# The products' weights at the start of their tile: an encoder block on one Trainium2 core

## The chip, the cores and the metric

The kernel runs on one core of one Trainium2 chip. The metric is the time of one execution on the device, in microseconds (us). Three executions of the kernel before took 967.39, 967.70 and 967.99 us; the median is 967.7. One further execution was profiled.

The names of the profile are used throughout. PE is TensorE's matmul part and PEld its part that loads the stationary operand (the weights of the array); DVE is VectorE, ACT is ScalarE, POOL is GpSimd, and SP issues most of the DMAs. A matmul holds one operand still in the array (the stationary one, 128 x 128 here) and lets the other stream past it (the moving one, 512 or 256 columns here). PSUM is the memory that matmuls write to, SBUF the one that they read from. A line number as L1014 is that of the kernel's source.

## What is computed

One layer of an encoder over 256 positions and 2048 features: a mixing half (windowed attention and a Fourier group) and a feed-forward half. The change lies in the feed-forward half:

```python
D_MODEL, SEQ = 2048, 256
D_FF = 5504

def _conv_ffn(h, w_up, dw_w, dw_b, w_down):
    up = h @ w_up
    gate, val = up[..., :D_FF], up[..., D_FF:]
    gate = lax.conv_general_dilated(gate, dw_w, ..., feature_group_count=D_FF) + dw_b
    act = jax.nn.gelu(gate, approximate=False) * val
    return act @ w_down

x = x + jnp.concatenate([a, f], axis=-1) @ w_out
x = x + _conv_ffn(_rmsnorm(x, norm2_g), w_up, dw_w, dw_b, w_down)
return _rmsnorm(x, normf_g)
```

All inputs and the output are float32.

## The kernel before

**Matmuls by parts.** The matmuls of the large projections work on float32r, a type in which PE streams one column of the moving operand after the other in a single pass. To keep the accuracy of float32, each operand is split into a high part (`hi`, the value copied to float32r) and a low part (`lo`, what the copy lost), and three of the four partial products are summed: high by high, low by high, high by low. ScalarE writes `hi`, VectorE subtracts and writes `lo`. For weights both go into one tile of the tag `parts`, of which there are three buffers, taken in turn (L139). A tile holds 2 x 2048 + 128 elements a partition: the high part in its first half, the low part in its second, and 128 spare elements. So each part can begin some elements in from the start of its half. `PLACES` (L136) gives these two offsets, in elements of 4 bytes, by the kind of unit:

- `still`, offsets 0 and 16: weights that are the stationary operand (query and key projections, and all up tiles). `still_weights` (L315) runs for each of 16 blocks a matmul of 512 columns with the high part (L320; the moving operand is the high and low part of the activations side by side) and one of 256 columns with the low part (L321).
- `first`, offsets 16 and 16: the first eight units, in which the weights are the moving operand.
- `moving`, offsets 0 and 0: the other units with moving weights: the output projection (`ps_a`, `ps_ff`) and the later parts of the down projection (`ps_l`, `ps_e`). `moving_weights` (L303) runs three matmuls of 512 columns a block (L309 to L311).
- `product`, offsets 28 and 28: the weights of the products, below.

**The feed-forward half.** The 43 blocks of 128 hidden features each have a gate tile and a value tile, 5504 = 43 x 128. Such an up tile is one unit of 1 MB of weights and 16 pairs of matmuls. The first 32 blocks form four groups of eight. For each group the down projection is not done as a plain matrix product: the group's activations, its weights and the output are cut into 2 x 2 blocks, and seven products of sums of blocks take the place of eight (Strassen's scheme in the form of Winograd). This is done for two halves of the output's columns, which makes 14 products a group and 56 in all. `by_parts` (L1010) runs a product: four blocks, each with three matmuls of 512 columns: L1014 (high operand, high weights), L1015 (low operand, high weights), L1016 (high operand, low weights). The operand `op` (from the activations) is stationary, the weights are the moving operand. The names of the products are P1, P2, P6, P7, N3, N4 and N5; the profile groups their tiles as `parts_P`, `parts_N`, `op_P`, `op_N`, `ps_P` and `ps_N`.

`split_product` (L904) makes the parts of a product's weights: a copy on ScalarE (L910) and a subtraction on VectorE (L911), then it starts the DMA or the accumulating DMA that prepares a later product's weights. Its source is one raw block of the weights or the tile `sumw`, in which sums of blocks are built.

**The order.** The order of work is written out by hand. The sixteen up tiles of the first eight blocks go first. Then come four stages; each runs the 14 products of a group of eight blocks together with the 16 up tiles of the next eight. `PATTERN` (L61) sets the order in a stage: three up tiles, then 13 times a product and an up tile, then a product. So 19 up tiles run ahead of the first product. At each item the parts of the item two places ahead are made (`ff_step`, L941), so that each writer waits for the buffer of `parts` that the item before has freed. Behind the four stages follow four units of the late down projection (`ps_l`), the last six up tiles, four more units `ps_l`, and the last down units (`ps_e`) with the final normalisation.

Of the kernel before, what the change touches and what calls it, by code (L numbers as in the profile page):

```python
# [83 lines left out]
def block_kernel(  # L84
# [48 lines left out]
    raws, halves = {}, {}  # L133


    PLACES = {"still": (0, 16), "first": (16, 16), "moving": (0, 0), "product": (28, 28)}  # L136

    def parts_tile(name, place):
        t = wp.tile([P, 2 * 2048 + 128], F32R, tag="parts", name=name, bufs=3)  # L139
        oh, ol = PLACES[place]  # L140
        return t[:, oh : oh + 2048], t[:, 2048 + ol : 4096 + ol]

    def load(i, pieces=1):
        if i < len(units) and i not in raws:
            src, n, _ = units[i]
            raws[i] = wp.tile([P, 2048], F32, tag="raw", name=f"raw{i}", bufs=RAW)
            m = n // pieces
            for p in range(pieces):
                s = slice(p * m, (p + 1) * m)
                nc.sync.dma_start(raws[i][:, s], src[:, s])  # L150
                yield
# [50 lines left out]
    first = load(0, 4)  # L202
# [1077 lines left out]
```

## Time and profile before

| | |
|---|---|
| median of three executions | 967.7 us |
| the profiled execution | 967.03 us |
| its span, first to last instruction | 965.3 us |
| mean granted clock of TensorE | 0.998 |
| up tiles alone, then the four stages of products with up tiles | about 260 to 367 us, 367 to 864 us of the span |
| HBM traffic | 208.65 MB read, 2.10 MB written |

The span is the time between the first and the last instruction of the profiled execution; what lies around it belongs to the execution as well. The busy time of an engine is the sum over its instructions. Records of matmuls overlap, since the next one begins to stream while the last one's results still drain; the time that a matmul costs is therefore not its record's duration but the step from its start to the next one's start. Rows in order of time give the start, the duration, the engine, the line and the tile; a row of a group gives the count, the busy time, the mean duration in nanoseconds and the idle time before its instructions.

### The profile page before, as it was taken

How to read it: one execution, taken by the hardware profiler on the slowest of the kernel's cores; microseconds unless marked ns; L12 is line 12 of the kernel's file. 1: busy time of each engine (PE TensorE's matmuls, PEld its weight loads, DVE VectorE, ACT ScalarE, POOL GpSimd, SP SyncE). 2: the span in 40 equal slices, each digit the busy share in tenths (PEclk: the TensorE clock that was granted, in tenths of full speed). 3: DMA queues.
4: the chain of work that ended last, by engine and by line, in shares of the span. 5: the costliest groups of instructions: out<-in, count | busy, mean ns of one | idle time of the engine just before them, and what ended most of it. 6: DMA issues, size and time to landing. Idle time of an engine off the chain costs nothing.

```text
span 965.3 us, 12801 instructions
## 1 busy us (share of the span) xinstructions
PE 955.1 (99%) x5089; PEld 820.1 (85%) x5089; DVE 745.0 (77%) x924; ACT 540.0 (56%) x654; POOL 44.6 (5%) x59
## 2 busy tenths in 40 slices
PE   9999999999999999999999999999999999999996
PEld 7789998888888888888888888888888888888885
DVE  5668877666576689787898877988778979878674
ACT  6756766554455446556565555665555655553534
POOL 0000000000000000000000000000000000000003
PEclk9999999999999999999999999999999999999999
DMA  8854444446456676977778787876977686775532
GB/s 320 338 189 155 175 138 168 142 167 215 177 177 243 233 220 194 288 226 256 225 253 240 235 293 231 261 236 206 290 245 245 206 278 213 227 225 210 209 132 88
DMA packets 33548, 211.59 MB, mean 219 GB/s; under 512 B 3792, under 2 KB 4304, under 8 KB 9424
## 3 DMA queue, kind: packets, MB, share of 16 engines
q1 hardware_dynamic: 29744, 184.54, 51.8%
q0 software_dynamic: 3600, 26.22, 14.5%
q8 instruction: 40, 0.66, 0.3%
q14 instruction: 20, 0.16, 0.0%
q10 hardware_dynamic: 144, 0.01, 0.0%
HBM read 208.65 MB, written 2.10 MB: 218 GB/s over the span
## 4 chain that ended last, share of the span: by engine, by line
PE 98%; DMA 1%; ACT 0%; SPq 0%; POOL 0%; issue 0%; DVE 0%; ACTq 0%; POOLq 0%
PE ps_val L320 16%; PE ps_gate L320 16%; PE ps_gate L321 8%; PE ps_val L321 8%; PE ps_q L320 5%; PE ps_P L1015 3%; PE ps_P L1014 3%; PE ps_P L1016 3%; PE ps_N L1015 2%; PE ps_q L321 2%; PE ps_N L1014 2%; PE ps_a L311 2%; PE ps_a L309 2%; PE ps_a L310 2%; PE ps_N L1016 2%; PE ps_k L320 2%
## 5 line engine op out<-in xcount | busy, mean ns | idle before, releaser
L171 DVE TENSOR_TENSOR parts<-raw,parts 128x2048 fp32r<-128x2048 f32 (+3 forms) x145 | 313.0, 2159 | 63.7 <-ACT parts L170 63.5
L170 ACT ACTIVATE parts<-raw 128x2048 fp32r<-128x2048 f32 (+3 forms) x144 | 262.0, 1819 | 75.4 <-PE ps_l L311 25.7
L320 PE MATMUL ps_gate<-hU,parts 128*128 128x512 f32 x688 | 242.2, 394 | 0.0
L320 PE MATMUL ps_val<-hU,parts 128*128 128x512 f32 x688 | 242.2, 394 | 0.0
L321 PE MATMUL ps_gate<-hU,parts 128*128 128x256 f32 x688 | 192.7, 280 | 0.0
L321 PE MATMUL ps_val<-hU,parts 128*128 128x256 f32 x688 | 192.7, 280 | 0.0
L320 PEld LDWEIGHTS ps_val<-hU,parts 128*128 128x128 f32 x688 | 129.3, 188 | 29.8
L320 PEld LDWEIGHTS ps_gate<-hU,parts 128*128 128x128 f32 x688 | 129.3, 188 | 29.7
L321 PEld LDWEIGHTS ps_gate<-hU,parts 128*128 128x128 f32 x688 | 129.2, 188 | 1.1
L321 PEld LDWEIGHTS ps_val<-hU,parts 128*128 128x128 f32 x688 | 129.1, 188 | 1.1
L805 ACT ACTIVATE ft_g<-ps_gate 128x256 f32<-128x256 f32 x43 | 16.6, 385 | 124.2 <-PE ps_gate L321 124.2
L805 ACT ACTIVATE ft_v<-ps_val 128x256 f32<-128x256 f32 x43 | 16.6, 386 | 97.5 <-PE ps_val L321 97.5
L320 PE MATMUL ps_q<-hT,parts 128*128 128x512 f32 x192 | 66.9, 393 | 0.0
L321 PE MATMUL ps_q<-hT,parts 128*128 128x256 f32 x192 | 53.2, 277 | 0.0
L1015 PE MATMUL ps_P<-parts_P,op_P 128*128 128x512 f32 x128 | 50.9, 398 | 0.0
L1014 PE MATMUL ps_P<-parts_P,op_P 128*128 128x512 f32 x128 | 50.2, 392 | 0.0
L1016 PE MATMUL ps_P<-parts_P,op_P 128*128 128x512 f32 x128 | 49.6, 387 | 0.0
L911 DVE TENSOR_TENSOR parts_N<-sumw,parts_N 128x2048 fp32r<-128x2048 f32 x16 | 36.6, 2290 | 10.1 <-ACT parts_N L910 10.1
L320 PEld LDWEIGHTS ps_q<-hT,parts 128*128 128x128 f32 x192 | 36.1, 188 | 7.3
L807 DVE TENSOR_TENSOR fa_g<-ps_gate,ft_g 128x256 f32<-128x256 f32 x43 | 18.1, 421 | 29.0 <-ACT ft_g L805 29.0
L1015 PE MATMUL ps_N<-parts_N,op_N 128*128 128x512 f32 x96 | 38.2, 398 | 0.0
L309 PE MATMUL ps_a<-parts,cat 128*128 128x512 f32 x96 | 37.9, 395 | 0.0
(323 smaller groups left out, 1591.9 us busy)
## 6 DMA issues: line engine op xcount, KB each, us to landing
raw<-in_w_up SPq DMA_DIRECT2D x86, 1024.0 KB, 5.0
raw<-in_w_in SPq DMA_DIRECT2D x21, 1024.0 KB, 5.0
raw<-in_w_out SPq DMA_DIRECT2D x16, 1024.0 KB, 4.8
sumw<-in_w_down POOLq DMA_DIRECT2D x16, 1024.0 KB, 8.6
raw<-in_w_down_late SPq DMA_DIRECT2D x8, 1024.0 KB, 4.8
raw<-in_w_down_last SPq DMA_DIRECT2D x4, 768.0 KB, 4.3
raw<-in_w_in SPq DMA_DIRECT2D x8, 256.0 KB, 6.6
xs<-in_x SPq DMA_DIRECT2D x4, 512.0 KB, 10.7
```

Source lines behind the costliest of these rows:

```text
L170: nc.scalar.activation(hi[:, s], raw[:, s], AF.Copy)
L171: nc.vector.tensor_tensor(lo[:, s], raw[:, s], f32(hi[:, s]), ALU.subtract)
L309: nc.tensor.matmul(ps, ah, wh, start=first and q == q0, stop=False)
L310: nc.tensor.matmul(ps, al, wh, start=False, stop=False)
L311: nc.tensor.matmul(ps, ah, wl, start=False, stop=last and q == q0 + len(kk) - 1)
L320: nc.tensor.matmul(ps, hi[:, s], h, start=k == 0, stop=False)
L321: nc.tensor.matmul(ps[:, 0:S], lo[:, s], h[:, 0:S], start=False, stop=k == NK - 1)
L805: nc.scalar.activation(tmp, ps[:, S : 2 * S], AF.Copy)
L911: nc.vector.tensor_tensor(lo, src, f32(hi), ALU.subtract)
L1014: nc.tensor.matmul(ps, o[:, 0, p, :], hi[:, s], start=first and p == 0, stop=False)
L1015: nc.tensor.matmul(ps, o[:, 1, p, :], hi[:, s], start=False, stop=False)
L1016: nc.tensor.matmul(ps, o[:, 0, p, :], lo[:, s], start=False, stop=last and p == 3)
```

## The change

The offsets of the kind `product` go from 28 to 0 elements, for the high and for the low part. The tile, its size, its buffers, and the offsets of all other kinds stay.

```diff
-    PLACES = {"still": (0, 16), "first": (16, 16), "moving": (0, 0), "product": (28, 28)}
+    PLACES = {"still": (0, 16), "first": (16, 16), "moving": (0, 0), "product": (0, 0)}
...
     def parts_tile(name, place):
         t = wp.tile([P, 2 * 2048 + 128], F32R, tag="parts", name=name, bufs=3)
         oh, ol = PLACES[place]
         return t[:, oh : oh + 2048], t[:, 2048 + ol : 4096 + ol]
```

## The prediction

> **What bounds the kernel now.** I read the page first, then the stages, then TensorE's instructions in order of time.
>
> ```profile
> span 965.3 us, 12801 instructions
> ...
> PE 955.1 (99%) x5089; PEld 820.1 (85%) x5089; DVE 745.0 (77%) x924; ACT 540.0 (56%) x654; POOL 44.6 (5%) x59
> ...
> PE 98%; DMA 1%; ACT 0%; SPq 0%; POOL 0%; issue 0%; DVE 0%; ACTq 0%; POOLq 0%
> ...
> 492.90:621.00 128.10, 128.10 (x680) 109.66 (x679) 106.93 (x109) 72.48 (x70) 5.26 (x6) 1.00 0.79 246
> 621.00:749.30 128.30, 128.30 (x681) 109.82 (x680) 107.21 (x109) 72.69 (x70) 5.25 (x6) 1.00 0.79 245
> ```
>
> The first three lines are the page's span, its busy times and its chain of waits. The last two come from the view by stages: start and end of the second and third group, length, then busy time of PE, PEld, DVE, ACT and POOL, then the granted clock and DMA. In these groups PE never stops, its clock is at full, VectorE works 107 of 128 us and ScalarE 73. So the time is the number of matmuls times the step from one to the next, and no other engine's gain or loss reaches the end unless it makes PE wait. The step is therefore what has to be read closely.
>
> ```profile
> 367.31 0.39 PE L1014 MATMUL ps_P<-parts_P,op_P 128*128 128x512 f32 x1
> 367.55 0.40 PE L1015 MATMUL ps_P<-parts_P,op_P 128*128 128x512 f32 x1
> 367.78 0.39 PE L1016 MATMUL ps_P<-parts_P,op_P 128*128 128x512 f32 x1
> ...
> 370.09 0.39 PE L320 MATMUL ps_val<-hU,parts 128*128 128x512 f32 x1
> ...
> 375.69 0.39 PE L1014 MATMUL ps_P<-parts_P,op_P 128*128 128x512 f32 x1
> ...
> 476.17 0.39 PE L1014 MATMUL ps_N<-parts_N,op_N 128*128 128x512 f32 x1
> ```
>
> These are PE's rows in order of time: start, duration, line. A product (12 matmuls of 512 columns) runs from 367.31 to 370.09: 2.78 us, a mean step of 0.231. The up tile behind it (16 pairs of 512 and 256 columns) runs to 375.69: 5.60 us, 0.350 a pair. 13 such product-and-tile periods end at 476.17: 108.86 / 13 = 8.37 us each, so the two numbers hold throughout. Now the same shapes after the groups, where the moving operand already lies without offset:
>
> ```profile
> 864.22 0.40 PE L309 MATMUL ps_l<-parts,act 128*128 128x512 f32 x1
> ...
> 866.54 0.39 PE L310 MATMUL ps_l<-parts,act 128*128 128x512 f32 x1
> ...
> 885.75 0.39 PE L309 MATMUL ps_l<-parts,act 128*128 128x512 f32 x1
> ...
> 886.43 0.39 PE L320 MATMUL ps_gate<-hU,parts 128*128 128x512 f32 x1
> ...
> 887.47 0.39 PE L320 MATMUL ps_gate<-hU,parts 128*128 128x512 f32 x1
> ...
> 891.89 0.39 PE L320 MATMUL ps_val<-hU,parts 128*128 128x512 f32 x1
> ...
> 919.09 0.39 PE L309 MATMUL ps_l<-parts,act 128*128 128x512 f32 x1
> ...
> 920.25 0.39 PE L311 MATMUL ps_l<-parts,act 128*128 128x512 f32 x1
> ...
> 920.48 0.39 PE L309 MATMUL ps_l<-parts,act 128*128 128x512 f32 x1
> ```
>
> Three steps from 885.75 to 886.43 take 0.68: 0.227 each, against 0.231 in the products. And five up tiles from 891.89 to 919.09 take 27.20: 5.44 each, 0.340 a pair, against 0.350, with the same hU, the same parts buffers, the same place and nothing waited for. So a pair has two paces, and which one it runs at is not fixed by its own addresses; it is handed on from the matmuls before. The groups' tiles are all on the slow one:
>
> ```profile
> L320 PE MATMUL ps_gate<-hU,parts 128*128 128x512 f32 x144 | 50.9, 396 | 0.0
> ...
> L320 PE MATMUL ps_gate<-hU,parts 128*128 128x512 f32 x48 | 16.5, 389 | 0.0
> ...
> 272.03 0.47 PE L320 MATMUL ps_gate<-hU,parts 128*128 128x512 f32 x1
> ```
>
> The first two are the gate's groups of instructions from 271.8 to 367 us and from 886.6 to 919 us: 396 ns a record ahead of the first product, 389 behind the last. The third row is where the slow pace begins: a record of 0.47 us behind four small matmuls. From there nothing interrupts PE, and the products with their offset of 28 do not lead it out.
>
> **The change, part by part.** It removes and adds no instruction, no wait and no DMA; the tile, its three buffers and the order stay. 112 bytes fall away from the address of both parts of a product's weights: ScalarE's write (L910), VectorE's read and write (L911), and the moving operand of L1014 to L1016. In the built program of before, the parts' three buffers begin at bytes 93984, 110880 and 127776 of a partition, all 288 past a multiple of 512; so do the operands' tiles, the act tiles and the cat tiles that are loaded as stationary weights, while the hT tiles are 96 past one. A product's moving rows thus go from 400 to 288, the same remainder as the weights loaded beside them. That is just the case of ps_l (moving 288, weights 288), so its rows price the products.
>
> Products, 56 of them: settled, 12 steps of 0.227 are 2.72 us. Coming from a fast up tile they start unsettled: from 919.09 to 920.25 the first five steps take 1.16 where settled ones take 1.13, so 0.03 more. 2.75 against 2.78 saves 0.03, times 56 is 1.7 us. Bounds for this step: settled from the first (0.06 saved, 3.4 us), or never (below).
>
> Up tiles behind the first product: four groups of 16 are 64, less the three ahead of the first product, 61. If a settled product hands the fast pace on, as ps_l does at 886.43, each saves 5.60 - 5.44 = 0.16, or 9.8 us. The way back into the pace costs: three pairs from 886.43 to 887.47 take 1.04 against 1.02, so 0.02 for each of the 55 tiles that follow a product directly, 1.1 us. Bounds: all 61 fast (9.8), or none (0).
>
> The first product meets a tile on the slow pace, for which no row exists. The nearest is ps_l at 864.22, which follows a product of offset 28: its first ten steps, to 866.54, take 2.32, 0.05 more than settled, and then it is settled. A product has twelve steps, so I take it that the first one, or at worst one of the next, gets through.
>
> The writers: is either slower at the new place?
>
> ```profile
> L171 DVE TENSOR_TENSOR parts<-raw,parts 128x2048 fp32r<-128x2048 f32 x130 | 297.3, 2287 | 56.0 <-ACT parts L170 55.9
> L170 ACT ACTIVATE parts<-raw 128x2048 fp32r<-128x2048 f32 x130 | 248.9, 1915 | 60.8 <-PE ps_l L311 16.8 <-PE ps_a L311 14.2 <-PE ps_ff L311 9.2
> ...
> L911 DVE TENSOR_TENSOR parts_N<-sumw,parts_N 128x2048 fp32r<-128x2048 f32 x16 | 36.6, 2290 | 10.1 <-ACT parts_N L910 10.1
> ...
> L910 ACT ACTIVATE parts_N<-sumw 128x2048 fp32r<-128x2048 f32 x16 | 30.6, 1911 | 0.0
> ```
>
> The offset-free and offset forms differ by 4 ns, at most 56 x 0.004 = 0.2 us on engines with 16 to 43% idle: nothing on the path. What hides the writers is that they run two items ahead of PE. A faster PE eats into that cover. Its thinnest place:
>
> ```profile
> 817.32 2.28 DVE L911 TENSOR_TENSOR parts_N<-sumw,parts_N 128x2048 fp32r<-128x2048 f32 x1
> ...
> 820.05 0.39 PE L1016 MATMUL ps_N<-parts_N,op_N 128*128 128x512 f32 x1
> ```
>
> After eight sums in a row VectorE ends these low parts at 819.60; PE reads them first at 820.05, 0.45 later. In the two tiles and the product ahead of it PE will gain about 0.16 + 0.03 + 0.16 = 0.35, so some 0.1 is left. Should it be gone, PE waits a tenth or two, and one tile may fall back to the slow pace (0.16): under 0.4 us, in the range. VectorE's 107 us still fit in the new group, 128.3 less about 2.6.
>
> Sum: 1.7 + 9.8 - 1.1 = 10.4 us. The profiled execution took 967.03 us (965.3 span and 1.7 around it), 0.7 under the median of 967.7 of the runs shown; on that scale 967.7 - 10.4 = **957.3 us**. With rows to 0.01 us, 56 and 61 times, and with the entry costs dropped (13.2 in all) or doubled (about 7.6), the likeliest case alone lies from 954.5 to 960.
>
> A rule of the Trainium skill speaks against all this. "TensorE: Matmul & The Clock Gate", Step-by-step: what each phase is for, says that PE reads the moving operand and the weights through two independent ports, and that "Loading the next tile's weights doesn't steal SBUF read bandwidth from the running matmul." By it, where the operands lie could not matter and the change would be worth 0 us. The trace does not agree as far as it shows: 0.340 and 0.350 for the same pair, 0.227 and 0.231 for the same shape.
>
> **The rivals.** *The tiles fall back.* The products settle but each gate or value tile returns to 0.350. Against it: 886.43 to 891.89, where the tile stays fast. For it: 272.03, where a fast stage went slow behind other matmuls. Then every product enters from the slow side and costs 2.77: 56 x 0.01, 967.1 us.
>
> *Half.* The pace is lost at waits or some entries and won back only later; about half the tiles gain: 967.7 - 5.2 = 962.5 us.
>
> *No effect of the place.* The two paces come from something that the change does not touch, and the products' 0.231 is their own: 967.7 us. For it: nothing in the page names addresses. Against it: the late products of the same shape, with another place, do not show them.
>
> *Slower: the products lock on their longest step.* The hi and lo operands are 2048 bytes apart here, 1024 in act and cat. If that keeps moving rows and loaded weights colliding when both have the remainder 288, all twelve steps could be as long as the longest of now:
>
> ```profile
> L1014 PE MATMUL ps_P<-parts_P,op_P x128: 392/392/393, 367.3 to 855.2; 128*128 128x512 f32 x128
> ...
> L1015 PE MATMUL ps_P<-parts_P,op_P x128: 398/398/398, 367.5 to 855.4; 128*128 128x512 f32 x128
> ...
> L1016 PE MATMUL ps_P<-parts_P,op_P x128: 387/387/388, 367.8 to 855.6; 128*128 128x512 f32 x128
> ```
>
> These rows of the view of the tile give the shortest, median and longest record. Steps go with these durations: the longest is 6 ns above the mean of 392. 12 x 0.006 x 56 adds 4.0 us, with the tiles still slow: 971.7 us. It decides as soon as the mean step passes 0.231. Against it: the three buffers of the parts lie at different multiples of 512 from the weights, and over all of them the shortest and longest record of a line are 0 or 1 ns apart, so a multiple of 512 between two operands counts for nothing here.
>
> **How the numbers follow.** The forecast 0.74, half 0.08, falling back 0.08, no effect 0.05, slower 0.05. A measurement of this kernel tells about 0.2% (1.9 us) from no change: the first two are faster (0.82), the next two the same (0.13), the last slower (0.05). The range from 954.5 to 963.5 holds the forecast with both its bounds, and the half case.
>
> **What would show it.** Right: L1014 to L1016 all near 389 ns once settled, L320 of the groups near 389 instead of 395, a product-and-tile period of 8.21 us, and the first ps_l some 10 us earlier. If the products show 389 but L320 stays at 395, the handing on failed; if L1014 to L1016 keep 392, 398 and 387, the place is not what sets them; if all show 398, they locked. Idle time on PE in the groups would mean that VectorE's cover broke.

## The result and the profile after

| | before | after |
|---|---|---|
| median | 967.85 us (967.39 to 968.18, 4 runs) | 957.66 us (957.35 to 959.19, 4 runs) |
| ratio | 1 | 0.9898, 95% interval 0.9881 to 0.9915 |
| span of the profiled execution | 965.3 us | 957.4 us |

The change saves 10.2 us, 1.0%; 957.3 had been forecast. The same page of the kernel after, its span, busy times and chain of waits:

```profile
span 957.4 us, 12801 instructions
...
PE 947.1 (99%) x5089; PEld 814.9 (85%) x5089; DVE 745.3 (78%) x924; ACT 540.2 (56%) x654; POOL 44.6 (5%) x59
...
PE 93%; DMA 3%; DVE 1%; ACT 1%; issue 1%; SPq 0%; POOL 0%; ACTq 0%; POOLq 0%
```

The same instructions, the same work on the other engines, and 8 us less on PE. The profiled execution of after is the longest of the four, and its chain holds more DMA than before (3% against 1%): its first loads came later, so that its first product starts at 369.31 us instead of 367.31. That lies ahead of what the change touches: in a second profile of the same kernel the first product starts at 367.58 us. What the change does is read behind that point. PE in order of time (start, duration, line), from the first product on:

```profile
369.31 0.40 PE L1014 MATMUL ps_P<-parts_P,op_P 128*128 128x512 f32 x1
...
372.08 0.39 PE L320 MATMUL ps_val<-hU,parts 128*128 128x512 f32 x1
...
377.54 0.39 PE L1014 MATMUL ps_P<-parts_P,op_P 128*128 128x512 f32 x1
...
380.28 0.39 PE L320 MATMUL ps_gate<-hU,parts 128*128 128x512 f32 x1
...
385.75 0.39 PE L1014 MATMUL ps_N<-parts_N,op_N 128*128 128x512 f32 x1
...
476.02 0.39 PE L1014 MATMUL ps_N<-parts_N,op_N 128*128 128x512 f32 x1
...
856.36 0.39 PE L309 MATMUL ps_l<-parts,act 128*128 128x512 f32 x1
```

The first product takes 2.77 us (before 2.78), the tile behind it at once 5.46 instead of 5.60. The second product takes 2.74. 13 periods of a product and a tile end at 476.02: 106.71 / 13 = 8.21 us, against 8.37. From the first product to the first `ps_l` it is 487.05 us against 496.91 (864.22 less 367.31 in the rows of before): 9.9 us of the 10.2 lie in this stretch.

The records say the same. The gate's group of instructions (count, busy time, mean ns), first of before from 367.3 to 864.2 us, then of after from 369.3 to 856.3 us; behind them the products' lines of after in the view of the tile (shortest, median and longest record):

```profile
L320 PE MATMUL ps_gate<-hU,parts 128*128 128x512 f32 x481 | 169.7, 395 | 0.0
```

```profile
L320 PE MATMUL ps_gate<-hU,parts 128*128 128x512 f32 x481 | 165.7, 390 | 0.0
```

```profile
L1014 PE MATMUL ps_P<-parts_P,op_P x128: 388/393/399, 369.3 to 847.5; 128*128 128x512 f32 x128
L1015 PE MATMUL ps_P<-parts_P,op_P x128: 388/390/398, 369.5 to 847.7; 128*128 128x512 f32 x128
L1016 PE MATMUL ps_P<-parts_P,op_P x128: 388/390/397, 369.8 to 847.9; 128*128 128x512 f32 x128
```

The tiles' 512-column matmuls went from 395 ns to 390. The products no longer repeat one pattern of 392, 398 and 387; they run from 388 to 399, since each begins unsettled and settles on the way.

The thinnest place of VectorE's cover did break, by a little. VectorE's and PE's rows of after there:

```profile
810.55 2.28 DVE L911 TENSOR_TENSOR parts_N<-sumw,parts_N 128x2048 fp32r<-128x2048 f32 x1
```

```profile
812.53 0.40 PE L1015 MATMUL ps_N<-parts_N,op_N 128*128 128x512 f32 x1
812.89 0.51 PE L1016 MATMUL ps_N<-parts_N,op_N 128*128 128x512 f32 x1
```

The low parts are ready at 812.83, and the step to the matmul that reads them is 0.36 instead of about 0.23. This product takes 3.02 us by its starts, 0.27 more than the others: 0.13 is the wait, the rest lies in the steps behind it, which are longer again. The tile behind the product, at 5.47, comes back to the fast pace.

### The profile page after: what moved, and what is told of

It is laid out like the page before. It is cut to its first block, busy times and chain, and to the rows that moved or that the text cites. A ratio compares the mean times of both kernels' runs of the same rounds, so it can differ in the third digit from the quotient of the medians.

```text
span 957.4 us, 12801 instructions
## 1 busy us (share of the span) xinstructions
PE 947.1 (99%) x5089; PEld 814.9 (85%) x5089; DVE 745.3 (78%) x924; ACT 540.2 (56%) x654; POOL 44.6 (5%) x59
## 4 chain that ended last, share of the span: by engine, by line
PE 93%; DMA 3%; DVE 1%; ACT 1%; issue 1%; SPq 0%; POOL 0%; ACTq 0%; POOLq 0%
PE ps_gate L320 16%; PE ps_val L320 16%; PE ps_gate L321 8%; PE ps_val L321 8%; PE ps_q L320 5%; PE ps_P L1015 3%; PE ps_P L1014 3%; PE ps_P L1016 3%; DMA raw<-in_w_in 3%; PE ps_q L321 2%; PE ps_a L311 2%; PE ps_a L309 2%; PE ps_a L310 2%; PE ps_N L1015 2%; PE ps_N L1014 2%; PE ps_N L1016 2%
## 5 line engine op out<-in xcount | busy, mean ns | idle before, releaser
L171 DVE TENSOR_TENSOR parts<-raw,parts 128x2048 fp32r<-128x2048 f32 (+3 forms) x145 | 313.2, 2160 | 63.4 <-ACT parts L170 63.4
L320 PE MATMUL ps_gate<-hU,parts 128*128 128x512 f32 x688 | 238.2, 391 | 0.0
L320 PE MATMUL ps_val<-hU,parts 128*128 128x512 f32 x688 | 238.1, 391 | 0.0
L1015 PE MATMUL ps_P<-parts_P,op_P 128*128 128x512 f32 x128 | 50.2, 392 | 0.0
L1016 PE MATMUL ps_P<-parts_P,op_P 128*128 128x512 f32 x128 | 49.9, 390 | 0.0
L911 DVE TENSOR_TENSOR parts_N<-sumw,parts_N 128x2048 fp32r<-128x2048 f32 x16 | 36.6, 2290 | 10.1 <-ACT parts_N L910 10.1
L1015 PE MATMUL ps_N<-parts_N,op_N 128*128 128x512 f32 x96 | 37.7, 393 | 0.0
```

Of the source, the lines that this page charges most:

```text
L171: nc.vector.tensor_tensor(lo[:, s], raw[:, s], f32(hi[:, s]), ALU.subtract)
L320: nc.tensor.matmul(ps, hi[:, s], h, start=k == 0, stop=False)
L911: nc.vector.tensor_tensor(lo, src, f32(hi), ALU.subtract)
L1015: nc.tensor.matmul(ps, o[:, 1, p, :], hi[:, s], start=False, stop=False)
L1016: nc.tensor.matmul(ps, o[:, 0, p, :], lo[:, s], start=False, stop=last and p == 3)
```

## Experiments

Each run is one profiled execution, with the kernel before timed on the same chip (966.6 to 967.8 us); of e11 five executions were timed, of the kernel after beside it (e12) four. Executions of one kernel lie up to 1.8 us apart, so a small difference between single ones says little; the products and tiles decide. Their times are differences of starts in PE's rows; the first product behind the slow pace and the one that waits for VectorE can be longer than the table has it.

| run | products' offset (high, low), elements | product us | tile us | time us |
|---|---|---|---|---|
| before | 28, 28 | 2.775 | 5.60 | 966.6 to 968.2 |
| after | 0, 0 | 2.745 | 5.46 | 957.7 |
| e1 | 128, 128 | 2.745 | 5.46 | 957.12 |
| e2 | 64, 64 | 2.745 | 5.46 | 958.53 |
| e5 | 32, 32 | 2.80 twice, then 2.78 | 5.60 once, then 5.47 | 960.15 |
| e3 | 16, 16 | 2.75 | 5.60 | 966.56 |
| e6 | 16, 16, operands moved along | 2.746 | 5.454 | 957.50 |
| e9 | 0, 28 | 2.77 to 2.79 | 5.60, 5.44, 5.60 in turn | 965.17 |
| e10 | 28, 128 | 2.78, 2.74 in turn | 5.46, 5.60 in turn | 963.01 |
| e4 | 0 in the first stage, then 28 | 2.745, then 2.720 | 5.46, then 5.440 | 956.40 |
| e7 | 0 in the first product, then 28 | 2.771, then 2.720 | 5.462, then 5.440 | 954.25 |
| e8, e11 | 28, one up tile at 80 | 2.720 | 5.440 | 953.06, 952.29 |

**Is it the remainder, or the start of the tile?** An offset of 128 elements is 512 bytes; 64, 16 and 32 elements, in the other runs, are 256, 64 and 128 bytes.

```diff
-... "product": (0, 0)}
+... "product": (128, 128)}
```

What was expected of e1, e2, e3 and e5, in this order:

> The products' parts lie 128 elements (512 bytes) into their tile instead of 0, so the moving rows have the remainder 288 by 512 again, as the weights loaded beside them. Theory (the place relative to the loaded weights by 512 bytes sets the step): as the kernel after, products with a settled step of 0.227 us and up tiles at 0.340 a pair behind the first product, 957 to 959 us. Rival (the distance from the start of the tile counts, or two writers and readers disturb each other by absolute place): as the kernel before, steps of 0.231 and pairs of 0.350, 967 to 968 us.

> Offset 64 elements, 256 bytes off the remainder of the loaded weights. Theory in its narrow form (only equal remainders by 512 settle at 0.227): a step other than 0.227 and tiles at 0.350, about 967 us. Wide form (a period of 256 or less; the first eight units of the kernel before have moving rows 256 bytes off their weights and settle at 0.227): as the kernel after, 957 to 959 us.

> Offset 16 elements, 64 bytes off. If the period is 64 bytes or less: as the kernel after, 957 to 959 us. If it is larger: a product step of its own, between 0.227 and 0.238, and the up tiles on one of their two paces; at 0.350 a pair about 967 us. Rival (only a start that is a multiple of 64 bytes off matters, as 28 elements are not): 957 to 959 us too, so this run tells only together with the one at 64 elements and those that follow.

> Offset 32 elements, 128 bytes off the loaded weights. The offset of 256 bytes did as 0 did, that of 64 did not. If the period is 128 bytes: as the kernel after, products of 2.745 us and up tiles of 5.46, 957 to 959 us. If it is 256: as at 64 bytes, products of 2.74 to 2.78 us and tiles left at 5.60, about 966.5 us.

512 and 256 bytes did just as 0: products of 2.745 us, tiles of 5.46, first tile behind the first product included. 128 bytes is a place of its own, and neither of its two expectations came true: the first tile behind a product still takes 5.60 us, the second product leads to the fast pace, and from there products take 2.78 us and the tiles behind them 5.47. 64 bytes leaves the tiles on the slow pace with somewhat shorter products. So the start of the tile is nothing special, and the three places 0, 256 and 512 bytes off are alike; those 64, 112 and 128 bytes off are not.

**Is it the place of the moving rows, or of the one operand against the other?** A tile of 16 elements a partition at the head of the feed-forward half's pool moves everything in that pool by 64 bytes. Of what PE reads in the products and the up tiles, only the operands `op` lie there; the products' weights go to offset 16 with them:

```diff
     hT[:] = hT2
+    fp.tile([P, 16], F32, tag="pad", name="pad", bufs=1)
     r2b = fp.tile([P, S], F32, tag="r2b", name="r2b", bufs=1)
...
-... "product": (0, 0)}
+... "product": (16, 16)}
```

What was expected:

> Offset 16 elements as in the run at 966.6 us, but everything of the feed-forward half's own pool, so the operands loaded beside the products' weights too, lies 64 bytes further on: moving rows and loaded weights have one remainder again, 352. Theory (what counts is the place of the one against the other): products settle and lead the tiles to 5.44 to 5.46 us, 957 to 960 us, the late down units (now 64 bytes off their act tiles) perhaps a little slower. Rival (the absolute place of the moving rows counts): products of 2.748 us and tiles of 5.60, about 966.5 us.

PE in order of time, first of e3 (16 elements, operands not moved), then of this run (L1015 is here the product's first line):

```profile
376.66 0.40 PE L1014 MATMUL ps_P<-parts_P,op_P 128*128 128x512 f32 x1
...
379.41 0.39 PE L320 MATMUL ps_gate<-hU,parts 128*128 128x512 f32 x1
...
385.01 0.40 PE L1014 MATMUL ps_N<-parts_N,op_N 128*128 128x512 f32 x1
```

```profile
407.73 0.40 PE L1015 MATMUL ps_P<-parts_P,op_P 128*128 128x512 f32 x1
...
410.48 0.40 PE L320 MATMUL ps_gate<-hU,parts 128*128 128x512 f32 x1
...
415.93 0.40 PE L1015 MATMUL ps_N<-parts_N,op_N 128*128 128x512 f32 x1
```

The product takes 2.75 us in both; the tile takes 5.60 in the one and 5.45 in the other, and the whole 966.56 and 957.50 us. The products' moving rows lie at the same place, and of PE's operands only those loaded beside them have moved. What counts is the place of the one operand against the other. The late down units show it from the other side: in this run their `act` tiles are moved and their weights not, and the four units from the first `ps_l` on take 22.51 us instead of 22.23, the four behind the last up tiles 22.39 instead of 21.79.

**Does every product have to lie there, and does it hand its pace on?** In the first of these runs (e4) only the first stage's products are at 0, in the second (e7) only the very first product.

```diff
-... "product": (0, 0)}
+... "product": (0, 0), "shifted": (28, 28)}
...
-        hi, lo = ... = parts_tile(f"parts_{p}_{g}{c}", "product")
+        hi, lo = ... = parts_tile(
+            f"parts_{p}_{g}{c}", "shifted" if g else "product"
+        )
```

```diff
-            f"parts_{p}_{g}{c}", "shifted" if g else "product"
+            f"parts_{p}_{g}{c}", "product" if (g, c, p) == (0, 0, "P1") else "shifted"
```

What was expected of e4, and then of e7:

> Only the 14 products of the first stage lie without an offset, the other 42 at 28 elements as before. Theory (each product hands its own pace on to the tile behind it, whatever came before): the first stage gains about 2.5 us, and from the first product of the second stage on products step at 0.231 and tiles pair at 0.350, as in the kernel before: 964.5 to 966 us. Rival (one push out of the slow pace is enough, and the fast one then holds): tiles stay at 0.340 in all four stages, only the products' own 0.03 us each are lost: 958.5 to 960.5 us.

> Only the very first product lies without an offset, all 55 others at 28 elements. Theory as it now stands (a product at 28 keeps whichever pace it meets, a product at 0 leads to the fast one): the first takes 2.77 us, all others 2.720, and the tiles 5.440, some 0.6 us less than with the whole first stage at 0: 955.5 to 956.5 us. Rival (one product is too short to settle from the slow pace, its twelve steps being just enough): tiles back at 5.60 behind it, 967 us.

In e4 the theory fell. The rival's mechanism held, the tiles stay fast in all four stages, but not its price: it had the products at 28 lose 0.03 us each and the time at 958.5 to 960.5 us, and they gain instead. The time was 956.40 us, and the stretch from the first product to the first `ps_l` 485.29 us against 487.05 with all products at 0. Rows of PE in e4 (L1016 is here a product's first line), in the first stage at offset 0 and in the second at 28:

```profile
376.49 0.39 PE L1016 MATMUL ps_P<-parts_P,op_P 128*128 128x512 f32 x1
...
379.24 0.39 PE L320 MATMUL ps_gate<-hU,parts 128*128 128x512 f32 x1
...
384.70 0.39 PE L1016 MATMUL ps_N<-parts_N,op_N 128*128 128x512 f32 x1
...
502.22 0.39 PE L1016 MATMUL ps_P<-parts_P,op_P 128*128 128x512 f32 x1
...
504.94 0.39 PE L320 MATMUL ps_gate<-hU,parts 128*128 128x512 f32 x1
...
510.38 0.39 PE L1016 MATMUL ps_N<-parts_N,op_N 128*128 128x512 f32 x1
```

At 0 a product takes 2.75 and the tile 5.46; at 28 they take 2.72 and 5.44, not the 2.78 and 5.60 of the kernel before. A product at 28 has two paces as well, and here it keeps the one that it meets. A product at 0 leads to the fast pace from either, but pays for it each time: 0.025 us in itself and 0.021 in the tile behind. The theory formed from this priced the run with one product at 0 before it ran, at 955.5 to 956.5 us; its products and tiles came out as written (2.771 for the first, then 2.720 and 5.440), and its time, 954.25, a little under: its first product began at 366.69 us, 1.6 us earlier than the 368.26 of e4.

**Is the pace set ahead of all products?** The kernel before with its offsets of 28, and one change: the weights of the third up tile, the one behind the four small matmuls, lie 80 elements in (288 + 320 = 608, remainder 96, as hU's rows).

```diff
-            units.append((w_up[...], 2048, "still"))
+            units.append((w_up[...], 2048, "level" if n == 2 else "still"))
...
-... "product": (28, 28)}
+... "product": (28, 28), "level": (80, 80)}
```

What was expected of the one profile (e8), of its five executions (e11) and of the kernel after beside them (e12):

> The kernel before with all products at 28 elements; only the third up tile's weights (the first tile behind the four small matmuls, where the slow pace begins) lie 80 elements in, so that the loaded weights have the remainder 96 of the moving rows beside them. Theory (equal remainders settle from any start, and everything behind keeps the pace): that tile at 16 x (0.227 + 0.120) = 5.55 us, then 16 more tiles ahead of the first product at 5.44 instead of 5.60, products at 2.720, tiles at 5.44: 967.7 - 2.6 - 3.1 - 9.7 = 952 to 953.5 us. Rival (the tile settles, but the next one with offsets 0 and 16 falls to the slow pace again): 967 us.

> The kernel before with the one up tile at 80 elements again, now timed in five rounds: 952.5 to 953.5 us, a ratio of 0.985 to the kernel before, and 4 to 5 us less than the kernel after.

> The kernel after, timed in five rounds beside it: 957 to 958 us.

PE of e8: the third tile and its successor, then groups of instructions from 278.5 to 851 us.

```profile
272.91 0.48 PE L320 MATMUL ps_gate<-hU,parts 128*128 128x512 f32 x1
...
278.55 0.39 PE L320 MATMUL ps_val<-hU,parts 128*128 128x512 f32 x1
...
283.99 0.39 PE L320 MATMUL ps_gate<-hU,parts 128*128 128x512 f32 x1
```

```profile
L320 PE MATMUL ps_gate<-hU,parts 128*128 128x512 f32 x609 | 209.0, 389 | 0.0
...
L1014 PE MATMUL ps_P<-parts_P,op_P 128*128 128x512 f32 x128 | 49.8, 389 | 0.0
L1015 PE MATMUL ps_P<-parts_P,op_P 128*128 128x512 f32 x128 | 49.8, 389 | 0.0
L1016 PE MATMUL ps_P<-parts_P,op_P 128*128 128x512 f32 x128 | 49.8, 389 | 0.0
```

The third tile takes 5.64 (5.55 had been expected; its first step is the long one behind the small matmuls), the next 5.44, and from there the groups of 512 columns stand at 389 ns: the products at 28 elements too, which had 392, 398 and 387 in the kernel before. Five executions have a median of 952.29 us, a ratio of 0.9849 (0.9836 to 0.9863), beside four of the kernel after with 957.72 us, 0.9903 (0.9889 to 0.9916). That is a little less than the 952.5 to 953.5 us expected, and 5.4 us below the kernel after instead of 4 to 5. This version beats both: 14.7 us for the place of one tile of 1 MB.

Two things that the traces show limit this. VectorE's cover at the thinnest place shrinks further as PE gets faster: there the product of e8 takes 3.14 us, 0.42 more than the others. And not every interruption loses the pace. Behind that product the tile is back on the fast pace after four pairs, and in the kernel before, behind eight small matmuls shortly ahead of those that lose it, a tile settles by itself:

```profile
806.23 0.39 PE L1014 MATMUL ps_N<-parts_N,op_N 128*128 128x512 f32 x1
...
809.37 0.40 PE L320 MATMUL ps_val<-hU,parts 128*128 128x512 f32 x1
...
810.75 0.39 PE L320 MATMUL ps_val<-hU,parts 128*128 128x512 f32 x1
...
811.43 0.39 PE L320 MATMUL ps_val<-hU,parts 128*128 128x512 f32 x1
```

```profile
264.76 0.47 PE L320 MATMUL ps_val<-hU,parts 128*128 128x512 f32 x1
...
266.23 0.39 PE L320 MATMUL ps_val<-hU,parts 128*128 128x512 f32 x1
...
266.57 0.39 PE L320 MATMUL ps_val<-hU,parts 128*128 128x512 f32 x1
```

The first rows are of e8, the others of before; in both the first four pairs take longer (1.38 and 1.47 us against 1.36), and from the fifth on a pair takes 0.340. What makes one interruption lose the pace and another not was not found. In the kernel before, 7 of the 16 query and key tiles, with the same offsets and small matmuls between them, also run at 0.350, and no run changed those.

**Which of the two parts does it?** One part at the remainder of the loaded weights, the other at 28 elements.

```diff
-... "product": (0, 0)}
+... "product": (0, 28)}
```

```diff
-... "product": (0, 0)}
+... "product": (28, 128)}
```

What was expected of e9, and then of e10:

> Of each product's parts only the high one moves to the start (remainder 288, as the loaded weights); the low one keeps 28 elements (400). Eight of a product's twelve steps then have equal remainders. If each such step pushes the pace on and the others hold it: tiles led to 5.44 to 5.47 us, products between 2.72 and 2.77, 954 to 959 us. If both parts have to move: tiles at 5.60, 966 to 968 us.

> The other way round: the high part keeps 28 elements (remainder 400), the low part lies at 128 elements (remainder 288 again). Four of a product's twelve steps have equal remainders. If each such step pushes: the fast pace is reached too, if only after some products, 954 to 960 us. If the high part's eight steps decide: tiles at 5.60, 966 to 968 us.

Neither side of either expectation came true. With the low part at 28 a tile in three was fast, with the high part at 28 every other. PE of the second of these runs (e10):

```profile
367.78 0.39 PE L1014 MATMUL ps_P<-parts_P,op_P 128*128 128x512 f32 x1
...
370.56 0.40 PE L320 MATMUL ps_val<-hU,parts 128*128 128x512 f32 x1
...
376.02 0.39 PE L1014 MATMUL ps_P<-parts_P,op_P 128*128 128x512 f32 x1
...
378.77 0.39 PE L320 MATMUL ps_gate<-hU,parts 128*128 128x512 f32 x1
...
384.36 0.39 PE L1014 MATMUL ps_N<-parts_N,op_N 128*128 128x512 f32 x1
```

The tiles take 5.46 and then 5.59. In this run a product that meets the slow pace leads out of it, and one that meets the fast pace leads back. So the steps at 28 do not merely hold the pace when they are mixed with others, and with one part at 28 and the other at the remainder the tiles do not stay fast. What a mixed sequence does is read from a run, not from counting equal steps.

## Why the prediction was right

**The bound and the step.** In the four stages PE stayed without a pause but for one wait of about 0.13 us, and the gain is in its steps. That held.

**Products.** 2.75 from 2.78 was forecast and 2.745 from 2.775 measured, 56 x 0.030 = 1.7 us, of which the product with the wait took 0.27 back. The number held, but its reason was only half right. The prediction took the 0.231 of the products for a matter of their own place. The kernel with one tile at 80 elements has products at 28 and at 0.227: the 0.231 was the slow pace of this shape, and the place at 0 is by itself 0.025 us a product dearer than the place at 28 on the fast pace. What was a saving in the sum is really the way out of the slow pace, less a price. The sum did not need to know this, since it took both its ends, 2.78 and 2.75, from rows.

**Tiles.** 5.46 was forecast for a tile behind a product (5.44 and 0.02 for the way back) and 5.46 measured, for all of the stretch: 61 tiles with a mean of 5.460 against 5.599 make 8.5 us, where 9.8 - 1.1 = 8.7 had been written. The handing on, the step with the least behind it, held from the first product: twelve steps were enough to settle from the slow pace.

**Writers and cover.** The prediction compared L911 with L171 as forms with and without an offset, though most rows of L171 write a low part that lies 16 elements in. After settles it: at offset 0, L911 and L910 kept their 2.29 and 1.91 us:

```profile
L911 DVE TENSOR_TENSOR parts_N<-sumw,parts_N 128x2048 fp32r<-128x2048 f32 x16 | 36.6, 2290 | 10.1 <-ACT parts_N L910 10.1
L910 ACT ACTIVATE parts_N<-sumw 128x2048 fp32r<-128x2048 f32 x16 | 30.6, 1910 | 0.0
```

The cover at the thinnest place was put at 0.1 us and turned out just gone; the loss of 0.27 lies within the 0.4 that had been set for it.

**The rivals.** The place without effect is ruled out: one product moved by 112 bytes, nothing else changed, was worth 13 us (e7), and the loaded operands moved by 64 bytes beside unmoved rows 9 us (e6 against e3). This is the case of the Trainium skill's rule in "TensorE: Matmul & The Clock Gate", Step-by-step: what each phase is for, that loading weights takes no read bandwidth from the running matmul. What the prediction drew from it, that the place could not matter, does not hold for these float32r matmuls, whose pace changed by 3% with it; whether it is the loading that takes something from them, no view shows. The products did not lock on their longest step, and the tiles fell back neither all nor by half: all 61 were fast.

**What stays open.** Which part of the chip makes the two paces was not measured; no view names it. The runs show two things that decide between them (the place of one operand against the other, and what ran before), not why, and not what every interruption or mixed sequence leads to.

## What to carry to other kernels

Where one engine never pauses, read its step from start to start and compare it between stretches of the same shape: a difference of 3% with nothing waited for was 10 to 15 us here. A step can depend on what ran before, so an offset that was found by trial with one history may be right or wrong with another; first find where the pace is lost and set it there, which here was worth 14.7 us against 9.3 for moving the weights of all products behind it. An ablation that changes all places at once would have put the gain down to 56 products; the runs with one of them show that one was enough.

## What was not expected of the hardware

- Matmuls of one shape with the same operands and places have two stable paces (0.340 and 0.350 us a pair of 512 and 256 columns, 2.720 and 2.775 us a product at 28 elements), and held either for hundreds of microseconds where nothing interrupted them.
- Products whose moving rows lie 0, 256 or 512 bytes off the remainder of the loaded operand, with both parts, led to the fast pace from either, within twelve steps of 512 columns.
- Such a product has a price of its own: about 0.025 us at its beginning and 0.021 in the tile behind it, so that one is better than 56.
